# FFN-down of a decoder layer: one operand sum of a seven-product square made by a plain and an accumulating DMA into a ring, two operands in one subtraction, and 7, 7, 7, 5 such squares instead of 7, 7, 7, 4

## The chip, the core and the metric

The kernel runs on one NeuronCore of one Trainium2 chip. TensorE (PE) multiplies matrices, VectorE (DVE) and ScalarE (ACT) work elementwise, GpSimd (POOL) and SyncE (SP) issue transfers here, and 16 DMA engines move the bytes. The metric is device time of one launch in microseconds (us), lower is better. Matmuls accumulate in PSUM; everything else that is named below lies in SBUF.

## What is computed

One layer of a hybrid decoder for 256 tokens of width 2048, in float32: a mixer (multi-scale pooling beside RWKV-7), a squared-ReLU MLP of width 8192, a gate fed by a per-layer embedding, and a final norm. The change lies in the MLP's second product, and only there:

```python
h2 = rms_norm(x, mlp_norm[i])
x = x + jnp.square(jax.nn.relu(h2 @ w_ffn_up[i])) @ w_ffn_down[i]      # (256, 8192) @ (8192, 2048)

gate = jax.nn.sigmoid(rms_norm(x, ple_norm[i]) @ w_ple_gate[i])
x = x + gate * (p[i] @ w_ple_proj[i])
return rms_norm(x, final_norm)
```

## The kernel before, in words

**Two halves per operand.** Every float32 operand of a product is split into a rounded part and a rest (`split_sb`, L171; `halves_of`, L1233; `split_w`, L161): ACT copies it to the reduced matmul type, DVE subtracts that copy from the original. A product is then three matmuls (high by high, high by low, low by high), written by `prod` (L1225). All of them have a 128x128 stationary operand (activations) and a 128x512 moving operand (weights).

**Order of the work.** The FFN runs in two halves of 4096 hidden columns (`ffn_half`, L1302). Each half first makes eight activation tiles `y` (`gemm_wide`, L1098, lines L1112 and L1117), and then runs two sweeps (`down_sweep`, L1207), one for each 1024 output columns. A sweep visits 16 squares. A square is 256 rows of the weight by the 1024 columns of the sweep, seen as four 128x512 blocks w11, w12, w21, w22, against four 128x128 activation blocks a11, a21, a12, a22. The four sweeps are called d00, d01, d10, d11 here (half, then column pair).

**Plain and seven-product squares.** A plain square costs 8 products, 24 matmuls. A seven-product square (Winograd's form of Strassen's product, called a seven below) costs 7 products, 21 matmuls, but needs sums. The sums of activations, s1 to s4, are made once per half in `activation_sums` (L1191) and kept in the tiles `S`. The sums of weight blocks are made in each sweep: t1 = w12 - w11, t3 = w22 - w12, t2 = t3 + w11, t4 = w21 - t2, four DVE subtractions of 128x512 each (L1269 to L1272) into the tile `td`, and then split. The tuple `SEVEN` (L1188) names the seven odd squares that are done so in d00, d01 and d10; d11 has four of them, 1, 3, 7 and 11.

**Tiles and their buffers.** Weights come in by `load_raw` (L149) on the SP queue, two tiles `raw` of 512 KB per square, in six buffers (three of tag `raw`, three of `raw2`). The queue issues in order, so a load whose buffer isn't free holds those behind it. Split weights lie in three pairs of tiles `wh`, `wl`; a seven also uses one tile `wa` and two tiles of tag `graw`. In d11 four calls of `keep` (L1167, at the visits 5, 8, 11 and 14) load blocks of the next stage's gate weight, each through one of the same two `graw` tiles, and split them into tiles that are kept. Buffers of one tag are handed out in turn, in program order.

**Who sets the order.** In this part of the kernel the instructions are put in order by the compiler's list scheduler, by program order and by the `high_priority` sections; each engine then runs its list in order and waits at semaphores. POOL builds masks and moves tiles early in the program and does nothing in the FFN.

**After the last seven** of a sweep (L1284) DVE combines the banks of products 1, 5, 6, 7 into the residual `xr`, scaled by `s2`; in d11 half of the transposes of `xr` for the next stage follow there (`h3_part`).

Of the kernel before, what the change touches and what calls it, by code (L numbers as in the profile page):

```python
# [9 lines left out]
F32 = mybir.dt.float32  # L10
F32R = mybir.dt.float32r
# [29 lines left out]
def trunk(  # L41
# [1114 lines left out]
    def inv_ms():  # L1156
        ss2 = rms_stat(xr, "n2")
        nc.vector.tensor_scalar(s2, ss2, 1.0 / D, NORM_EPS, op0=ALU.mult, op1=ALU.add)
        nc.vector.reciprocal(s2, s2)

    h3_box = []

# [24 lines left out]

    SEVEN = (1, 3, 5, 7, 9, 11, 13)  # L1188
    s_slots = (0, 2, 5)

    def activation_sums(box, kp, r):  # L1191

        i = SEVEN.index(kp)
        if i % 2 == 0:
            st = a8(s_slots[i // 2], f"S{kp}", F32R) if i < 6 else fp.tile([128, 1024], F32R, tag="S", name=f"S{kp}")
# [6 lines left out]
        nc.vector.tensor_tensor(s3, a11, a21, op=ALU.subtract)  # L1202
        nc.vector.tensor_tensor(s2_, s1, a11, op=ALU.subtract)
        nc.vector.tensor_tensor(s4, a12, s2_, op=ALU.subtract)
        split_sb(st[:, 0:512], st[:, 512:1024], t_[:, 0:512])

    def down_sweep(hf, pair, ys, sboxes, hooks=(), between=None, seven=SEVEN):  # L1207

        nm = f"d{hf}{pair}"
        hooks = dict(hooks)  # L1210
# [12 lines left out]
        left = dict(todo)  # L1223

        def prod(n, a_, w_):  # L1225
            first, last = left[n] == todo[n], left[n] == 1
            left[n] -= 1
            (ah, al), (wh, wl) = a_, w_
            nc.tensor.matmul(banks[n], ah, wh, start=first, stop=False)  # L1229
            nc.tensor.matmul(banks[n], ah, wl, start=False, stop=False)  # L1230
            nc.tensor.matmul(banks[n], al, wh, start=False, stop=last)  # L1231

        def halves_of(src, name, own=False):  # L1233

            pool, kw = (fp, dict(bufs=2)) if own else (wp, {})
            wh = pool.tile([128, 1024], F32R, tag="graw" if own else "wh", name=f"wh_{name}", **kw)
            wl = pool.tile([128, 1024], F32R, tag="graw" if own else "wl", name=f"wl_{name}", **kw)
            with tc.high_priority(20000):
                for c in range(2):
                    nc.scalar.activation(wh[:, c * 512 : c * 512 + 512], src[:, c * 512 : c * 512 + 512], AF.Copy)  # L1240
                nc.vector.tensor_tensor(wl, src, wh.bitcast(F32), op=ALU.subtract)
# [6 lines left out]
        def add(tt, c, src):  # L1248
            nc.vector.scalar_tensor_tensor(xs(tt, c), src, s2[:, tt : tt + 1], xs(tt, c), op0=ALU.mult, op1=ALU.add)

        for q, kp in enumerate(((0, 2, 1, 4, 3, *range(5, 16)) if hf else (0, 2, 1, 4, 3, 6, 5, 8, 7, 10, 9, 12, 11, 14, 13, 15)) if pair else range(16)):
            if q in hooks:
                hooks[q]()
            y, j = ys[kp // 2], kp % 2 * 512
            a11, a21, a12, a22 = ((y[:, j + i * 128 : j + i * 128 + 128], y[:, 1024 + j + i * 128 : 1152 + j + i * 128]) for i in range(4))
            rx, ry = (load_raw(w_down[pair, hf * 32 + 2 * kp + i], 1024, f"{nm}_{kp}_{i}") for i in range(2))
            if kp in seven:
                i = SEVEN.index(kp)
                st = sboxes[kp][:, i % 2 * 1024 : i % 2 * 1024 + 1024]
                s1, s2_, s3, s4 = ((st[:, c * 128 : c * 128 + 128], st[:, 512 + c * 128 : 640 + c * 128]) for c in range(4))  # L1260
                t_ = a8(1, f"t{nm}_{kp}")
                t1, t3, t2, t4 = (t_[:, c * 512 : c * 512 + 512] for c in range(4))
                wa = fp.tile([128, 1024], F32R, tag="wa", name=f"wa{nm}_{kp}")
                w11 = wa[:, 0:512], wa[:, 512:1024]
                with tc.high_priority(20000):
                    split_sb(*w11, rx[:, 0:512])
                w21, w22 = halves_of(ry, f"{nm}_{kp}b")
                with tc.high_priority(20000):
                    nc.vector.tensor_tensor(t1, rx[:, 512:1024], rx[:, 0:512], op=ALU.subtract)  # L1269
                    nc.vector.tensor_tensor(t3, ry[:, 512:1024], rx[:, 512:1024], op=ALU.subtract)  # L1270
                    nc.vector.tensor_tensor(t2, t3, rx[:, 0:512], op=ALU.add)
                    nc.vector.tensor_tensor(t4, ry[:, 0:512], t2, op=ALU.subtract)  # L1272
                w1, w3 = halves_of(t_[:, 0:1024], f"{nm}_{kp}c")
                w2, w4 = halves_of(t_[:, 1024:2048], f"{nm}_{kp}d", True)
                for n, a_, w_ in (("1", a11, w11), ("2", a12, w21), ("3", s4, w22), ("5", s1, w1), ("7", s3, w3), ("6", s2_, w2), ("4", a22, w4)):
                    prod(n, a_, w_)
            else:
                w11, w12 = halves_of(rx, f"{nm}_{kp}a")
                for n, a_, w_ in (("2", a11, w11), ("4", a21, w11), ("3", a11, w12), ("x", a21, w12)):
                    prod(n, a_, w_)  # L1280
                w21, w22 = halves_of(ry, f"{nm}_{kp}b")
                for n, a_, w_ in (("2", a12, w21), ("4", a22, w21), ("3", a12, w22), ("x", a22, w22)):
                    prod(n, a_, w_)
            if kp == seven[-1]:  # L1284
                u = fp.tile([128, 512], F32, tag="r", bufs=2, name=f"u{nm}")
                with tc.high_priority(20000):
                    add(0, 0, b1)
                    nc.scalar.activation(u, b1, AF.Copy)
                    nc.vector.tensor_tensor(u, b6, u, op=ALU.add)
                    add(0, 1, b5)  # L1290
                    add(1, 1, b5)
                    add(0, 1, u)
                    nc.vector.tensor_tensor(u, b7, u, op=ALU.add)
                add(1, 0, u)
                add(1, 1, u)
                if between is not None:
                    between()
        for n, tt, c in (("2", 0, 0), ("4", 1, 0), ("3", 0, 1), ("x", 1, 1)):
            with tc.high_priority(30000):
                add(tt, c, banks[n])  # L1300

    def ffn_half(hf):  # L1302
# [26 lines left out]
        if hf == 0:  # L1329
            down_sweep(hf, 1, ys, sboxes)  # L1330
        else:
            down_sweep(hf, 1, ys, sboxes, {5: keep, 8: keep, 11: keep, 14: keep}, lambda: [h3_part("ple_norm", n) for n in range(2)], (1, 3, 7, 11))
# [9 lines left out]
    ph, pl = (fp.tile([128, 512], F32R, tag=nm, name=nm) for nm in ("ph", "pl"))  # L1342
    split_sb(ph, pl, praw[:, 0:512])
    pp = [a8(1 + tt, f"pp{tt}") for tt in range(2)]
    for n in range(4):
# [74 lines left out]
def _layout(i):  # L1420
# [13 lines left out]
    def ktiles(w):  # L1434
# [30 lines left out]
        "w_ffn_down": a["w_ffn_down"][0].reshape(64, 128, 2, 1024).transpose(2, 0, 1, 3),  # L1465
# [24 lines left out]
```

## Time and profile before

| what | value |
|---|---|
| runs of the kernel | 1180.1, 1182.39 and 1652.59 us, median 1182.39 |
| the execution that was profiled, its own time | 1180.25 us |
| its span from the first to the last instruction | 1178.2 us |
| DVE, ACT busy over the span | 873.3 us (74%), 709.3 us (60%) |
| sweeps d00 and d01, then d10 and d11, by TensorE's records | 557.9 to 722.5 us, 900.9 to 1069.6 us |
| sevens in the four sweeps | 7, 7, 7, 4 |

The profile is one execution. Its tables give busy time by engine, the span in 40 slices, the chain of work that ended last, groups of equal instructions, and waits with what ended them; a view by windows gives busy time of each engine in a stretch of the span, and a timeline lists the instructions of one engine with start, duration and, in brackets, the idle time ahead. A matmul of 128x512 is shown with 0.39 us, but matmuls are pipelined: what one costs in a full stream is the distance of two starts. Names with numbers left out stand for all tiles of that name (`raw_d` is every weight tile of FFN-down; `wl_d_6a` the low halves of the first weight tile of square 6).

### The profile page before, as it was taken

What the parts mean: (1) busy time and instruction counts of PE and PEld (TensorE: products, weight loads), DVE (VectorE), ACT (ScalarE), POOL (GpSimd) and SP (SyncE); (2) the same over time, 40 slices, a digit from 0 to 9 for tenths busy, and PEclk for the clock granted to TensorE, in tenths of its full rate; (3) what the DMA queues carried; (4) which work ended last, traced back from release to release, by engine and by line L of the source; (5) the groups of instructions that cost most, each with busy time, mean ns of one, the idle gap of its engine ahead of it and who ended that gap; (6) DMA issues with size and microseconds to landing.
All of it is one profiled execution on the core that took longest, in us unless ns stands there. A gap on an engine that the chain in (4) does not pass through costs nothing.

```text
span 1178.2 us, 17287 instructions
## 1 busy us (share of the span) xinstructions
PE 1162.5 (99%) x6419; PEld 973.4 (83%) x6419; DVE 873.3 (74%) x1188; ACT 709.3 (60%) x1309; POOL 13.7 (1%) x73
## 2 busy tenths in 40 slices
PE   8999999999999999999999999999999999999997
PEld 8787777788887888888888888888888888888886
DVE  7786996964656666767988987676668879788543
ACT  7776848676545565555665664555556655568543
POOL 2100000000000000000000000000000000000000
PEclk9999999999999999999999999999999999999999
DMA  7464343354465555555556556555555555767511
GB/s 290 154 202 146 135 140 119 119 179 157 160 203 178 177 182 196 184 192 200 187 204 212 198 202 209 186 191 191 185 195 190 202 205 195 290 233 249 197 56 72
DMA packets 60756, 216.81 MB, mean 184 GB/s; under 512 B 6784, under 2 KB 7552, under 8 KB 60288
## 3 DMA queue, kind: packets, MB, share of 16 engines
q1 hardware_dynamic: 60240, 214.99, 52.5%
q8 instruction: 50, 0.82, 0.3%
q10 hardware_dynamic: 432, 0.73, 0.2%
q14 instruction: 34, 0.28, 0.1%
HBM read 213.59 MB, written 2.10 MB: 183 GB/s over the span
## 4 chain that ended last, share of the span: by engine, by line
PE 96%; ACT 1%; DVE 1%; DMA 0%; issue 0%; SPq 0%; POOL 0%; DVEq 0%; POOLq 0%
PE u_w L1112 20%; PE u_w L1117 10%; PE d_b L1231 7%; PE d_b L1229 7%; PE d_b L1230 7%; PE d_w L1231 2%; PE d_w L1229 2%; PE d_w L1230 2%; PE gt_b L242 2%; PE gt_b L241 2%; PE gt_b L238 2%; PE zk_b L241 1%; PE zk_b L242 1%; PE o_b L241 1%; PE o_b L242 1%; PE zv_b L238 1%
## 5 line engine op out<-in xcount | busy, mean ns | idle before, releaser
L1112 PE MATMUL u_w<-h,wh_u 128*128 128x512 f32 x1024 | 321.9, 395 | 0.0
L167 ACT ACTIVATE wh_u<-raw_u 128x512 fp32r<-128x512 f32 x256 | 147.5, 623 | 160.9 <-issue 98.2
L168 DVE TENSOR_TENSOR wl_u<-raw_u,wh_u 128x1024 fp32r<-128x1024 f32 x128 | 156.6, 1224 | 105.2 <-ACT wh_u L167 103.5
L1117 PEld LDWEIGHTS u_w<-h,wl_u 128*128 128x128 f32 x1024 | 192.4, 188 | 45.4
L1117 PE MATMUL u_w<-h,wl_u 128*128 128x256 f32 x1024 | 201.4, 278 | 0.0
L1112 PEld LDWEIGHTS u_w<-h,wh_u 128*128 128x128 f32 x1024 | 156.0, 189 | 0.1
L168 DVE TENSOR_TENSOR wl_gt<-raw_gt,wh_gt 128x1024 fp32r<-128x1024 f32 x24 | 29.4, 1224 | 23.2 <-ACT wh_gt L167 23.2
L167 ACT ACTIVATE wh_gt<-raw_gt 128x512 fp32r<-128x512 f32 x48 | 28.0, 638 | 23.1 <-PE gt_b L242 14.4
L241 PE MATMUL gt_b<-wh_gt,h 128*128 128x512 f32 x96 | 37.3, 389 | 0.0
L242 PE MATMUL gt_b<-wh_gt,h 128*128 128x512 f32 x96 | 37.3, 389 | 0.0
L168 DVE TENSOR_TENSOR wl_o<-raw_o,wh_o 128x1024 fp32r<-128x1024 f32 x16 | 19.6, 1222 | 12.9 <-ACT wh_o L167 9.9
L167 ACT ACTIVATE wh_o<-raw_o 128x512 fp32r<-128x512 f32 x32 | 18.4, 623 | 16.3 <-issue 8.5
L167 ACT ACTIVATE wh_zp<-raw_zp 128x512 fp32r<-128x512 f32 x32 | 18.6, 623 | 15.7 <-PE zp_b L242 7.2
L168 DVE TENSOR_TENSOR wl_zk<-raw_zk,wh_zk 128x1024 fp32r<-128x1024 f32 x16 | 19.4, 1220 | 10.4 <-ACT wh_zk L167 10.4
L241 PE MATMUL zk_b<-wh_zk,hTh 128*128 128x512 f32 x64 | 25.2, 394 | 1.4 <-ACT wh_zk L167 1.4
L241 PE MATMUL zv_b<-wh_zv,hTh 128*128 128x512 f32 x64 | 26.0, 406 | 0.0
L167 ACT ACTIVATE wh_zk<-raw_zk 128x512 fp32r<-128x512 f32 x32 | 18.4, 622 | 12.4 <-PE zv_b L242 4.0
L241 PE MATMUL zp_b<-wh_zp,hTh 128*128 128x512 f32 x64 | 25.7, 401 | 0.0
L238 PE MATMUL gt_b<-wl_gt,h 128*128 128x512 f32 x96 | 25.7, 389 | 0.0
L168 DVE TENSOR_TENSOR wl_zv<-raw_zv,wh_zv 128x1024 fp32r<-128x1024 f32 x16 | 19.4, 1218 | 8.2 <-ACT wh_zv L167 7.4
L241 PE MATMUL zr_b<-wh_zr,hTh 128*128 128x512 f32 x64 | 25.4, 397 | 0.0
L242 PE MATMUL zp_b<-wh_zp,hTl 128*128 128x512 f32 x64 | 25.0, 391 | 0.0
(840 smaller groups left out, 2963.9 us busy)
## 6 DMA issues: line engine op xcount, KB each, us to landing
raw_u<-in_w_ffn_up_dram SPq DMA_DIRECT2D x128, 512.0 KB, 3.5
raw_d<-in_w_ffn_down_dram SPq DMA_DIRECT2D x128, 512.0 KB, 4.3
raw_gt<-in_w_ple_gate_dram SPq DMA_DIRECT2D x24, 512.0 KB, 3.5
raw_zk<-in_w_in_dram SPq DMA_DIRECT2D x16, 512.0 KB, 3.7
raw_zr<-in_w_in_dram SPq DMA_DIRECT2D x16, 512.0 KB, 3.3
raw_zv<-in_w_in_dram SPq DMA_DIRECT2D x16, 512.0 KB, 3.3
raw_zp<-in_w_in_dram SPq DMA_DIRECT2D x16, 512.0 KB, 3.2
raw_o<-in_w_out_dram SPq DMA_DIRECT2D x16, 512.0 KB, 4.2
```

Of the source, the lines that this page charges most:

```text
L167: nc.scalar.activation(wh[:, a * 512 : (a + 1) * 512], raw[:, a * 512 : (a + 1) * 512], AF.Copy)
L168: nc.vector.tensor_tensor(wl, raw, wh.bitcast(F32), op=ALU.subtract)
L238: nc.tensor.matmul(banks[tt], ah[:, ts_], halves[a][1], start=False, stop=last)
L241: nc.tensor.matmul(banks[tt], ah[:, ts_], halves[a][0], start=i + a == 0, stop=False)
L242: nc.tensor.matmul(banks[tt], al[:, ts_], halves[a][0], start=False, stop=False)
L1112: nc.tensor.matmul(bank[:, ct, :].rearrange("p (s t) -> p s t", s=2), wh[:, cs[ct]], hl, start=k == 0, stop=False, skip_group_check=True,)
L1117: nc.tensor.matmul(bank[:, ct, 0:T], wl[:, cs[ct]], hl[:, 0, :], start=False, stop=k == 15, skip_group_check=True)
L1229: nc.tensor.matmul(banks[n], ah, wh, start=first, stop=False)
L1230: nc.tensor.matmul(banks[n], ah, wl, start=False, stop=False)
L1231: nc.tensor.matmul(banks[n], al, wh, start=False, stop=last)
```

## The change

The output columns of index c = 1 are computed with the opposite sign inside a seven. Then the four weight operands are p1 = w11 + w12 (in place of t1), t2 = p1 - w22, and w21 - t2 and w11 - t2 (in place of t4 and t3). The last two are one subtraction over 1024 columns, with t2 broadcast, written in place over the weight tile `rx`, which now holds w21 and w11 side by side. The sign is put right when the banks are added to the residual (`ns2` = -`s2`, and s3 with its sign turned).

p1 isn't made by DVE. POOL issues two transfers of 256 KB into a slot of `ring` (four slots of 128x512): a plain one of w12, and one of w11 that adds to what is there. Both read the weight from HBM again. `begin_sum` issues them for the square that is four sevens ahead, at the end of each seven; the first four are issued ahead of the FFN. In turn the tile `ry` of a seven brings only w22 (256 KB).

The products of a seven go in the order 1, 2, 3, 5, 6, 4, 7 (before: 1, 2, 3, 5, 7, 6, 4). `wa` holds the split t2, the `graw` tiles the two results of the wide subtraction. d11 has five sevens, 1, 3, 5, 9 and 11, and visits the squares 0, 2, 1, 4, 3, 6, 5, 7, 8, and on to 15. The weight is laid out for these loads on the host. `S` for square 13 becomes a larger tile, in which `ph` and `pl` of the next stage lie too.

```diff
-    def down_sweep(hf, pair, ys, sboxes, hooks=(), between=None, seven=SEVEN):
+    ring = a8(1, "ring")
...
+            squares_of[hf, pair] = (1, 3, 5, 9, 11) if last else SEVEN
+            visits_of[hf, pair] = (0, 2, 1, 4, 3, 6, 5, 7, 8, *range(9, 16)) if last else (range(16), (0, 2, 1, 4, 3, 6, 5, 8, 7, 10, 9, 12, 11, 14, 13, 15))[pair]
+    in_line = [(*hp, kp) for hp, visits in visits_of.items() for kp in visits if kp in squares_of[hp]]
...
+    def slot(n):
+        return ring[:, n % 4 * 512 : n % 4 * 512 + 512]
+
+    def begin_sum():
+
+        n = len(begun)
+        if n < len(in_line):
+            hf, pair, kp = in_line[n]
+            nc.gpsimd.dma_start(slot(n), w_down[pair, hf * 16 + kp, 1, :, 1, :])
+            nc.gpsimd.dma_start(slot(n), w_down[pair, hf * 16 + kp, 0, :, 1, :], accum_op=ALU.add)
+            begun.append(n)
...
-            rx, ry = (load_raw(w_down[pair, hf * 32 + 2 * kp + i], 1024, f"{nm}_{kp}_{i}") for i in range(2))
+            rx, ry = (panel(kp, c, f"{nm}_{kp}_{c}", 1 if c and kp in seven else 2) for c in range(2))
             if kp in seven:
...
-                t_ = a8(1, f"t{nm}_{kp}")
-                t1, t3, t2, t4 = (t_[:, c * 512 : c * 512 + 512] for c in range(4))
+                p1 = summed(hf, pair, kp)
+                t2 = ry[:, 512:1024]
                 wa = fp.tile([128, 1024], F32R, tag="wa", name=f"wa{nm}_{kp}")
-                w11 = wa[:, 0:512], wa[:, 512:1024]
+                w2 = wa[:, 0:512], wa[:, 512:1024]
+                w21, w11 = halves_of(rx, f"{nm}_{kp}a")
+                wh, wl = (wp.tile([128, 1024], F32R, tag=hl, name=f"{hl}_{nm}_{kp}b") for hl in ("wh", "wl"))
+                w22, w1 = ((wh[:, c : c + 512], wl[:, c : c + 512]) for c in (0, 512))
                 with tc.high_priority(20000):
-                    split_sb(*w11, rx[:, 0:512])
-                w21, w22 = halves_of(ry, f"{nm}_{kp}b")
-                with tc.high_priority(20000):
-                    nc.vector.tensor_tensor(t1, rx[:, 512:1024], rx[:, 0:512], op=ALU.subtract)
-                    nc.vector.tensor_tensor(t3, ry[:, 512:1024], rx[:, 512:1024], op=ALU.subtract)
-                    nc.vector.tensor_tensor(t2, t3, rx[:, 0:512], op=ALU.add)
-                    nc.vector.tensor_tensor(t4, ry[:, 0:512], t2, op=ALU.subtract)
-                w1, w3 = halves_of(t_[:, 0:1024], f"{nm}_{kp}c")
-                w2, w4 = halves_of(t_[:, 1024:2048], f"{nm}_{kp}d", True)
-                for n, a_, w_ in (("1", a11, w11), ("2", a12, w21), ("3", s4, w22), ("5", s1, w1), ("7", s3, w3), ("6", s2_, w2), ("4", a22, w4)):
+                    split_sb(*w22, ry[:, 0:512])
+                    split_sb(*w1, p1)
+                    nc.vector.tensor_tensor(t2, p1, ry[:, 0:512], op=ALU.subtract)
+                    t43 = rx.rearrange("p (r n) -> p r n", r=2)
+                    nc.vector.tensor_tensor(t43, t43, t2.unsqueeze(1).to_broadcast([128, 2, 512]), op=ALU.subtract)
+                    split_sb(*w2, t2)
+                w4, w3 = halves_of(rx, f"{nm}_{kp}d", True)
+                for n, a_, w_ in (("1", a11, w11), ("2", a12, w21), ("3", s4, w22), ("5", s1, w1), ("6", s2_, w2), ("4", a22, w4), ("7", s3, w3)):
                     prod(n, a_, w_)
+                begin_sum()
...
+    for _ in range(4):
+        begin_sum()
     ffn_half(0)
     ffn_half(1)
```

More of the change, by code (lines that the diff above doesn't have):

```diff
@@ L1159, in inv_ms @@
         nc.vector.reciprocal(s2, s2)
+        nc.vector.tensor_scalar_mul(ns2, s2, -1.0)
     h3_box = []
@@ L1189, in trunk @@
     s_slots = (0, 2, 5)
+    ns2 = const.tile([128, 2], F32, name="ns2")
     def activation_sums(box, kp, r):
@@ L1205, in activation_sums, with summed, down_sweep @@
         split_sb(st[:, 0:512], st[:, 512:1024], t_[:, 0:512])
-    def down_sweep(hf, pair, ys, sboxes, hooks=(), between=None, seven=SEVEN):
+    ring = a8(1, "ring")
+    squares_of = {}
+    visits_of = {}
+    for hf in range(2):
+        for pair in range(2):
+            last = hf + pair == 2
+            squares_of[hf, pair] = (1, 3, 5, 9, 11) if last else SEVEN
+            visits_of[hf, pair] = (0, 2, 1, 4, 3, 6, 5, 7, 8, *range(9, 16)) if last else (range(16), (0, 2, 1, 4, 3, 6, 5, 8, 7, 10, 9, 12, 11, 14, 13, 15))[pair]
+    in_line = [(*hp, kp) for hp, visits in visits_of.items() for kp in visits if kp in squares_of[hp]]
+    begun = []
+    def slot(n):
[7 more added lines that the diff above has]
+            begun.append(n)
+    def summed(*square):
+        return slot(in_line.index(square))
+    def down_sweep(hf, pair, ys, sboxes, hooks=(), between=None):
         nm = f"d{hf}{pair}"
+        seven, visits = squares_of[hf, pair], visits_of[hf, pair]
         hooks = dict(hooks)
@@ L1246, in xs, with add, panel @@
             return xr[tt][:, o : o + 512]
-        def add(tt, c, src):
-            nc.vector.scalar_tensor_tensor(xs(tt, c), src, s2[:, tt : tt + 1], xs(tt, c), op0=ALU.mult, op1=ALU.add)
-        for q, kp in enumerate(((0, 2, 1, 4, 3, *range(5, 16)) if hf else (0, 2, 1, 4, 3, 6, 5, 8, 7, 10, 9, 12, 11, 14, 13, 15)) if pair else range(16)):
+        def add(tt, c, src, scale=s2):
+            nc.vector.scalar_tensor_tensor(xs(tt, c), src, scale[:, tt : tt + 1], xs(tt, c), op0=ALU.mult, op1=ALU.add)
+        def panel(kp, c, name, rows):
+            return load_raw(w_down[pair, hf * 16 + kp, c, :, 0:rows].rearrange("p r n -> p (r n)"), rows * 512, name)
+        for q, kp in enumerate(visits):
             if q in hooks:
@@ L1279, in down_sweep @@
-                for n, a_, w_ in (("2", a11, w11), ("4", a21, w11), ("3", a11, w12), ("x", a21, w12)):
+                w21, w11 = halves_of(rx, f"{nm}_{kp}a")
+                for n, a_, w_ in (("2", a12, w21), ("4", a22, w21), ("2", a11, w11), ("4", a21, w11)):
                     prod(n, a_, w_)
-                w21, w22 = halves_of(ry, f"{nm}_{kp}b")
-                for n, a_, w_ in (("2", a12, w21), ("4", a22, w21), ("3", a12, w22), ("x", a22, w22)):
+                w22, w12 = halves_of(ry, f"{nm}_{kp}b")
@@ L1283, in down_sweep @@
+                for n, a_, w_ in (("3", a12, w22), ("x", a22, w22), ("3", a11, w12), ("x", a21, w12)):
                     prod(n, a_, w_)
-            if kp == seven[-1]:
+            if kp == max(seven):
                 u = fp.tile([128, 512], F32, tag="r", bufs=2, name=f"u{nm}")
@@ L1291, in down_sweep @@
                     add(1, 1, b5)
-                    add(0, 1, u)
+                    add(0, 1, u, ns2)
                     nc.vector.tensor_tensor(u, b7, u, op=ALU.add)
                 add(1, 0, u)
-                add(1, 1, u)
+                add(1, 1, u, ns2)
                 if between is not None:
@@ L1341, in trunk @@
     praw = load_raw(pT.rearrange("p a t -> p (a t)"), 512, "pT")
-    ph, pl = (fp.tile([128, 512], F32R, tag=nm, name=nm) for nm in ("ph", "pl"))
+    phl = fp.tile([128, 2048], F32R, tag="S", name="phl")
+    ph, pl = phl[:, 0:512], phl[:, 512:1024]
     split_sb(ph, pl, praw[:, 0:512])
```

9 lines of the change are left out of this document (4 added, 5 removed).

## The prediction

> **What bounds the kernel now.** I read the page first, its busy shares and the chain, to see which engine sets the end; then TensorE's waits; then the windows of the four sweeps.
>
> ```profile
> PE 1162.5 (99%) x6419; PEld 973.4 (83%) x6419; DVE 873.3 (74%) x1188; ACT 709.3 (60%) x1309; POOL 13.7 (1%) x73
> ...
> PE   8999999999999999999999999999999999999997
> ...
> PE 96%; ACT 1%; DVE 1%; DMA 0%; issue 0%; SPq 0%; POOL 0%; DVEq 0%; POOLq 0%
> ```
>
> TensorE is busy in nearly every slice and is 96% of the chain. Busy time of pipelined matmuls can hide small gaps, so the waits and windows decide:
>
> ```profile
> PE zk_b L241 <- ACT wh_zk L167: 1.4, 1, 1.4
> ...
> PE um L854 <- ACT R L818: 0.4, 1, 0.4
> ...
> 557.90:640.20 82.30, 82.30 (x365) 68.18 (x364) 71.35 (x83) 49.66 (x86) 0.00 (x0) 1.00 0.58 202
> 640.20:722.50 82.30, 82.30 (x364) 68.12 (x363) 72.22 (x82) 49.12 (x85) 0.00 (x0) 1.00 0.57 199
> 900.90:983.20 82.30, 82.30 (x366) 68.14 (x365) 71.34 (x83) 49.64 (x86) 0.00 (x0) 1.00 0.55 197
> 983.20:1069.60 86.40, 86.40 (x389) 71.13 (x388) 73.19 (x83) 55.24 (x101) 0.00 (x0) 1.00 0.71 252
> ```
>
> TensorE has nine kinds of wait in the whole program, the first and the last are shown; none names `d_b` or `d_w`, the banks of FFN-down. In the windows (columns: length; busy of PE, weight loads, DVE, ACT, POOL; clock; DMA share; GB/s) TensorE is busy for all of each sweep at full clock, DVE for 72.22 of 82.30 us. So the sweeps last as long as their matmuls do. DVE relief is worth nothing by itself; only fewer matmuls are, as long as nothing new comes late.
>
> **The change, part by part.** The execution profiled took 1180.25 us; its span is 1178.2, and 2.05 lie around it. It is 2.1 under the median of the three runs shown (1182.39) and 0.15 over the lowest.
>
> *Matmuls: -0.69 us.* One square of d11 becomes a seven.
>
> ```profile
> 655.90 0.39 PE L1229 MATMUL d_b<-wh_d_4a,y 128*128 128x512 f32 x1
> ...
> 661.35 0.39 PE L1229 MATMUL d_w<-wad,y 128*128 128x512 f32 x1
> ...
> 666.11 0.39 PE L1229 MATMUL d_b<-wh_d_6a,y 128*128 128x512 f32 x1
> ...
> 671.54 0.39 PE L1229 MATMUL d_w<-wad,y 128*128 128x512 f32 x1
> ```
>
> The plain square 4 takes 661.35 - 655.90 = 5.45 us (24 matmuls, 0.227 each), the seven 3 takes 4.76 (21): 0.69 us less. It is on the path in full. All other squares keep their kind, and the order of products costs TensorE nothing.
>
> *DVE and ACT: 0, hidden under TensorE.* Steps of DVE in the stream:
>
> ```profile
> 663.27 1.22 DVE L1241 TENSOR_TENSOR wl_d_6a<-raw_d,wh_d_6a 128x1024 fp32r<-128x1024 f32 x1
> 664.40 0.68 DVE L173 TENSOR_TENSOR wad<-raw_d,wad 128x512 fp32r<-128x512 f32 x1
> 665.00 1.22 DVE L1241 TENSOR_TENSOR wl_d_6b<-raw_d,wh_d_6b 128x1024 fp32r<-128x1024 f32 x1
> 666.14 0.68 DVE L1272 TENSOR_TENSOR td<-raw_d,td 128x512 f32<-128x512 f32 x1
> ...
> L172 ACT ACTIVATE wad<-raw_d 128x512 fp32r<-128x512 f32 x25 | 15.4, 618 | 3.7 <-DMA raw_d<-in_w_ffn_down_dram 3.7
> ```
>
> A 512-wide step is 0.60 us, a 1024-wide one 1.14. A seven before: five narrow (four sums, one split) and three wide: 6.42. After: four narrow (t2, and the splits of w22, p1, t2) and three wide (w21 with w11, the double subtraction, its split): 5.82. That is -0.60 for 25 sevens, and +3.54 where a plain square (two wide, 2.28) becomes one: -11.5 us in all, off the path. The wide subtraction with a repeated operand isn't in the trace; I take 1.14 like other wide steps, between that and two narrow ones, 1.20, as a repeated operand brings no more elements. ACT keeps seven narrow copies per seven; the new seven adds three, 3 x 0.62 = 1.9 us, hidden: ACT is busy for 55.24 of 86.40 us in d11. `ns2` is one tiny step.
>
> The margin of DVE over TensorE is what hides this. `wl_d_6a` ends at 664.49 and is read by square 6's second matmul, 0.23 after 666.11: 1.85 us. A seven's first product now needs a wide split in place of a narrow one (+0.54), and its split w22 and p1 must follow the same buffer pair; TensorE stalls only where a chain is late by more than about 1.85.
>
> *More bytes: 0.* A seven loads 512 + 256 KB on SP and 2 x 256 KB on POOL in place of 1024 KB: +256 KB. A sweep of 16 squares goes from 16,384 to 18,176 KB, of which 7 x 256 = 1,792 KB accumulate. At the DMA share of d01 (0.57) that gives 0.63 if accumulating costs as much as copying. d11 already runs at 0.71 and 252 GB/s, and there TensorE has no gap either. So the added load is covered up to that point.
>
> No row shows an accumulating transfer or one issued by POOL. Below, its cost is 0 (hidden); no gain is possible, as the chain has no DMA in it. Above: the share without accumulating bytes stays 0.57, and these bytes add 0.57 x 1792/16384 = 0.062 for each multiple f of a copy's price; the engines are full at f = 6.9. I take hidden, as d11's row lies between.
>
> The Trainium skill (Collectives: The Full Stack, the part on the bandwidth ceiling) says that an adding transfer needs two source reads, so about twice the read traffic; by that f = 2, an estimate, the share is 0.69 and the sum stays as it is. No run here shows it yet.
>
> *Waits on POOL: 0.* The second transfer of a sum must wait until the first has landed, and the first until DVE and ACT have read the slot. POOL is at 0.00 in every sweep above and nothing else is queued there, so these waits hold only later sums. Who waits for them is ACT and DVE at p1, and behind it everything on these two engines. Sevens start 671.54 - 661.35 = 10.2 us apart, so four ahead is 41 us, less some 5 us of a seven's own time.
>
> ```profile
> raw_d<-in_w_ffn_down_dram SPq DMA_DIRECT2D x128, 512.0 KB, 4.3
> ...
> L158 SPq DMA_DIRECT2D raw_d<-in_w_ffn_down_dram x25: 327/328/328, 641.8 to 698.6; - x25
> ```
>
> Two transfers in a row at the price of twice the bytes, 4.3 us each, are 8.6: about 27 us to spare. The first four have the whole first half of the FFN.
>
> Against this the Trainium skill (SBUF — State Buffer, "Who interferes with whom") warns that transfers issued by GpSimd can starve while DVE holds the port they share, but by inference spares two-input subtractions like those here. If they were not spared, the writing of descriptors would have only DVE's idle 12% of d01: an issue of SP's 0.33 us would stretch to 2.7, two transfers to 14, still under 36. That is why the late sum below gets a small chance.
>
> *`rx` held longer: 0.* Before, `rx` was free after t2; now only after the split of w4 and w3, which product 4 needs.
>
> ```profile
> 664.51 0.33 SPq L158 DMA_DIRECT2D raw_d<-in_w_ffn_down_dram  x1
> ...
> 671.79 1.15 ACT L1240 ACTIVATE wh_d_8a<-raw_d 128x512 fp32r<-128x512 f32 x2 [1.56 <-issue]
> ```
>
> The load three squares on (square 8, behind seven 3) moves to at most 661.35 + 5 x 0.68 = 664.75; the next load behind it left at 664.51 anyway. Landing after 4.3, at 669.1, it is 2.7 us ahead of its split at 671.79.
>
> *`graw` and the kept gate weights: +1.75 us.* This is where I expect a new wait. In turn the two `graw` tiles go to seven 3, the first kept block, and the next seven. Before, that was square 7, two plain squares later; now it is square 5, one plain square later.
>
> ```profile
> 1008.84 0.39 PE L1231 MATMUL d_b<-wh_d_3d,y 128*128 128x512 f32 x1
> ...
> 1009.03 0.35 SPq L1170 DMA_DIRECT2D graw<-in_w_ple_gate_dram  x1
> ...
> 1016.20 1.15 ACT L1174 ACTIVATE gk<-graw 128x512 fp32r<-128x512 f32 x2 [0.29 <-DMA graw<-in_w_ple_gate_dram]
> ...
> 1018.64 1.23 DVE L1241 TENSOR_TENSOR wl_d_7d<-td,wh_d_7d 128x1024 fp32r<-128x1024 f32 x1
> ...
> DMA to landing us min/median/max: 4.0/5.1/7.1
> ```
>
> The kept load leaves as seven 3's last matmul ends (1009.03), lands 7.17 us later, and the low half of the next seven's pair, in the same tile, is ready at 1019.87, that is 3.67 after the landing. Counted from the end of seven 3: ready at 7.17 + 3.67 = 10.84. TensorE gets to that matmul after 5.45 for the plain square, five products of 0.68 and one matmul: 9.08. It waits 1.76 us. With the median landing of 5.1 the tile is ready at 8.77, and there is no wait. Bounds for one place: 0 (4.0 to 5.1) to 1.76 (7.1). It comes up twice, since seven 9, the third kept block and seven 11 stand alike. I take 1.75 for the first, whose load stood beside the 1 MB load of the final norm's weights and still will, and 0 for the other.
>
> Sum: 1180.25 - 0.69 + 1.75 = 1181.3 us.
>
> **The rivals.**
>
> *No stall at all.* If the scheduler hands `graw` over otherwise, or the first kept load lands in 5.1: 1180.25 - 0.69 = 1179.6. For it: TensorE had no wait in four sweeps. Against: the row at 1016.20.
>
> *The fifth square gives nothing and the chains get tight.* In place and behind p1, a seven's weights come later than the 1.85 us of margin allow, by some 0.2 us each: 26 x 0.2 = 5.2, on top of the forecast 1186.5. For it: two more dependent steps in a row, and ACT waiting in order. Against: DVE has 0.6 us more per seven.
>
> *Slower: accumulating transfers fill the DMA engines.* Place: the 16 engines in all sweeps; it decides from f = 6.9 on. At f = 10 a sweep of 82.3 us lacks (10 - 6.9) x 0.062 x 82.3 = 15.8 us, and with 26 sevens (3.7 sweeps' worth) 59 us: 1240. For it: no such row exists. Against: it needs seven times a copy's price.
>
> *Slower: sums late.* From about 36 us for one sum's two transfers on, each seven waits for the excess; at 40 us, 4 x 26 = 104 us: 1285. For it: POOL's path is untried here. Against: rows of 4.3 us.
>
> **How the numbers follow.** Forecast with a kept-block wait: 0.46. No stall: 0.26. Tight chains: 0.20. DMA engines full: 0.05. Sums late: 0.02. The remaining 0.01 is a scatter towards faster. About 2% (24 us) is what a measurement of this kernel can tell from no change. No case reaches 24 us less, since that would take a hundred matmuls: faster 0.01, same 0.92, slower 0.07. The predicted time is the forecast's, 1181.3. The range goes from the no-stall sum less the 2.3 us between the two close runs (1180.1, 1182.39), 1177.3, to the tight case plus as much, 1188.8; it holds 0.92 and its ends are the bounds of the unknown costs.
>
> **What the profile after would show.** Right: 369 matmuls of FFN-down in d11, distances of 0.227, PE waits of FFN-down of one or two entries on `wl_d_5d` or `wl_d_11d`, about 1.8 us; DVE near 68 of 82.3 us in d01; DMA share there 0.63 to 0.70; both transfers of a sum landed some 25 us before p1 is split. Wrong: waits of TensorE in d00, d01 or d10, a DMA share near 1, or ACT or DVE waiting for `ring`. A `graw` handed out in another order would take my 1.75 away.

## The result, and the profile after

The changed kernel takes 1199.83 us (median of four runs, 1196.25 to 1201.42) beside 1182.35 us for the kernel before on the same chip: a ratio of 1.015, 95% interval 1.0116 to 1.0184. It is slower by about 17 us, inside 2%, and outside the range that was forecast. One run of the kernel before (1652.59 us) and one of an experiment below (1442.19 us) were far slower than the rest, and no ratio uses them.

The profiled execution took 1198.61 us, span 1196.9. The busy shares and the first entries of the chain, as on the page of before:

```profile
PE 1168.4 (98%) x6416; PEld 972.9 (81%) x6416; DVE 859.4 (72%) x1169; ACT 707.0 (59%) x1312; POOL 51.2 (4%) x125
...
PE 17%; DVE 2%; DMA 1%; issue 1%; ACT 0%; DVEq 0%; SPq 0%; ACTq 0%
```

DVE is busy for 14 us less, ACT for 2 less, and POOL, which issues the sums, is busy for 4%. TensorE issues 3 matmuls fewer, yet is busy for 6 us more. And the chain, TensorE for 96% before, now runs over DVE and DMA as well and can be followed only for some 20% of the span. The waits of TensorE say where (us in total, times, longest):

```profile
PE d_b L1259 <- DVE wl_d_11d L1270: 2.6, 1, 2.6
PE d_b L1259 <- DVE wl_d_5b L173: 2.3, 2, 1.2
PE d_b L1259 <- DVE wl_d_11b L173: 2.3, 3, 1.0
PE d_b L1259 <- DVE wl_d_7b L173: 1.9, 1, 1.9
...
PE d_b L1259 <- DVE wl_d_3b L173: 1.4, 1, 1.4
...
PE d_w L1259 <- DVE wl_d_3b L173: 0.8, 1, 0.8
PE d_b L1259 <- DVE wl_d_5d L1270: 0.7, 1, 0.7
```

Where no bank of FFN-down stood before, eight kinds of entry stand now (the eighth, 0.3 on `wl_d_9b`, is left out). Most name `wl_..b` at L173: the low halves of w22 and p1. The windows of the four sweeps (columns as in the prediction):

```profile
557.67:644.50 86.83, 83.85 (x366) 67.67 (x364) 69.48 (x79) 49.01 (x87) 10.09 (x14) 1.00 0.70 215
644.50:730.10 85.60, 83.32 (x365) 67.86 (x364) 67.75 (x76) 48.64 (x86) 10.05 (x14) 1.00 0.70 220
908.40:994.56 86.16, 83.60 (x365) 67.76 (x364) 69.48 (x79) 49.04 (x87) 10.06 (x14) 1.00 0.69 217
994.56:1088.00 93.44, 88.59 (x391) 71.92 (x389) 73.68 (x84) 56.58 (x106) 1.43 (x2) 0.98 0.66 229
```

d00, d01 and d10 take 4.5, 3.3 and 3.9 us more than 82.3, and d11, up to the first matmul of the next stage, 93.4 where it took 86.9. That is 18.2 of the 18.7 us by which the span grew. TensorE isn't busy in all of these windows any more, and in d11 the clock is at 0.98.

The cause of the first three shows on DVE's timeline in d01 (start, length, and in brackets the idle time ahead with what ended it), in three stretches, with one row each of TensorE and SP:

```profile
676.29 0.69 DVE L1304 TENSOR_TENSOR raw_d<-ring,raw_d 128x512 f32<-128x512 f32 x1 [3.64 <-DMA raw_d<-in_w_ffn_down_dram]
676.90 1.22 DVE L1270 TENSOR_TENSOR wl_d_5d<-raw_d,wh_d_5d 128x1024 fp32r<-128x1024 f32 x1
678.03 0.68 DVE L173 TENSOR_TENSOR wl_d_5b<-raw_d,wh_d_5b 128x512 fp32r<-128x512 f32 x1
678.64 0.68 DVE L173 TENSOR_TENSOR wl_d_5b<-ring,wh_d_5b 128x512 fp32r<-128x512 f32 x1
...
678.77 0.50 PE L1259 MATMUL d_b<-wl_d_5b,S 128*128 128x512 f32 x1 [1.25 <-DVE wl_d_5b L173]
...
680.37 1.22 DVE L1270 TENSOR_TENSOR wl_d_8b<-raw_d,wh_d_8b 128x1024 fp32r<-128x1024 f32 x1
...
681.62 0.33 SPq L158 DMA_DIRECT2D raw_d<-in_w_ffn_down_dram  x1
...
686.59 0.69 DVE L1304 TENSOR_TENSOR raw_d<-ring,raw_d 128x512 f32<-128x512 f32 x1 [2.13 <-DMA raw_d<-in_w_ffn_down_dram]
687.20 1.22 DVE L1270 TENSOR_TENSOR wl_d_7d<-raw_d,wh_d_7d 128x1024 fp32r<-128x1024 f32 x1
```

L1304 is t2 = p1 - w22. The one at 676.29 belongs to seven 7, and behind it on DVE stand three splits of seven 5: the scheduler put the next seven's t2 ahead of them. t2 waits 3.64 us for its own load of w22; the splits behind it need nothing from that load, and TensorE waits 1.25 us for them. DVE runs its list in order: the Trainium skill (TensorE: Matmul & The Clock Gate, the part on the array's architecture) calls ACT's and DVE's queues strictly first in, first out, and these rows agree.

The stretch closes on itself. From t2 at 676.29 DVE works until the second tile of the plain square 8 is split, at 681.59. That split frees a buffer; SP issues the load of w22 for seven 9 into it at 681.62; it has landed when t2 of seven 9 starts, at 686.59. That is 5.30 of work and 4.97 of landing, 10.3 us in all, as long as TensorE needs for a pair of squares (10.2). There is no slack in the loop, so each late landing stays.

In the kernel before, the four sums stood behind all splits of the seven before them. DVE there, a view of the same kind:

```profile
670.27 1.23 DVE L1241 TENSOR_TENSOR wl_d_5c<-td,wh_d_5c 128x1024 fp32r<-128x1024 f32 x1 [1.18 <-ACT wh_d_5c L1240]
671.53 0.69 DVE L1269 TENSOR_TENSOR td<-raw_d 128x512 f32<-128x512 f32 x1
```

Those sums stood in a `high_priority` section as t2 does now, so the priority alone doesn't say why the scheduler moved t2 ahead; no run shows that.

Two more views of the changed kernel are needed later: transfers with their size and median landing, and groups of DVE and POOL (busy, mean ns of one, idle ahead).

```profile
raw_d<-in_w_ffn_down_dram SPq DMA_DIRECT2D x102, 512.0 KB, 4.4
ring<-in_w_ffn_down_dram POOLq DMA_DIRECT2D x52, 256.0 KB, 5.2
raw_d<-in_w_ffn_down_dram SPq DMA_DIRECT2D x26, 256.0 KB, 4.8
```

```profile
L1306 DVE TENSOR_TENSOR raw_d<-raw_d,raw_d 128x1024 f32<-128x1024 f32 x26 | 31.6, 1217 | 0.0
L1229 POOL DMA_DIRECT2D ring<-in_w_ffn_down_dram x26 | 22.6, 870 | 124.9 <-DMA ring<-in_w_ffn_down_dram 124.9
L1304 DVE TENSOR_TENSOR raw_d<-ring,raw_d 128x512 f32<-128x512 f32 x26 | 18.0, 691 | 44.3 <-DMA raw_d<-in_w_ffn_down_dram 44.1
L1228 POOL DMA_DIRECT2D ring<-in_w_ffn_down_dram x26 | 14.9, 575 | 597.6 <-DVE wl_d_1b L173 446.5 <-PE o3a_b L238 75.9 <-DVE wl_d_3b L173 19.5
```

t2 waited 44.1 us for its load over the program; the wide subtraction waits for nothing.

### The profile page after: what moved, and what is told of

Same layout as the page of the kernel before. It is cut to its first block, busy times and chain, and to the rows that moved or that the text cites. A ratio compares the mean times of both kernels' runs of the same rounds, so it can differ in the third digit from the quotient of the medians.

```text
span 1196.9 us, 17313 instructions
## 1 busy us (share of the span) xinstructions
PE 1168.4 (98%) x6416; PEld 972.9 (81%) x6416; DVE 859.4 (72%) x1169; ACT 707.0 (59%) x1312; POOL 51.2 (4%) x125
## 5 line engine op out<-in xcount | busy, mean ns | idle before, releaser
L1304 DVE TENSOR_TENSOR raw_d<-ring,raw_d 128x512 f32<-128x512 f32 x26 | 18.0, 691 | 44.3 <-DMA raw_d<-in_w_ffn_down_dram 44.1
L167 ACT ACTIVATE wh_gt<-raw_gt 128x512 fp32r<-128x512 f32 x48 | 27.8, 631 | 23.1 <-PE gt_b L242 14.4
L1228 POOL DMA_DIRECT2D ring<-in_w_ffn_down_dram x26 | 14.9, 575 | 597.6 <-DVE wl_d_1b L173 446.5
L1306 DVE TENSOR_TENSOR raw_d<-raw_d,raw_d 128x1024 f32<-128x1024 f32 x26 | 31.6, 1217 | 0.0
L1229 POOL DMA_DIRECT2D ring<-in_w_ffn_down_dram x26 | 22.6, 870 | 124.9 <-DMA ring<-in_w_ffn_down_dram 124.9
L168 DVE TENSOR_TENSOR wl_zk<-raw_zk,wh_zk 128x1024 fp32r<-128x1024 f32 x16 | 19.4, 1221 | 10.1 <-ACT wh_zk L167 10.1
```

Of the source, the lines that this page charges most:

```text
L167: nc.scalar.activation(wh[:, a * 512 : (a + 1) * 512], raw[:, a * 512 : (a + 1) * 512], AF.Copy)
L168: nc.vector.tensor_tensor(wl, raw, wh.bitcast(F32), op=ALU.subtract)
L1229: nc.gpsimd.dma_start(slot(n), w_down[pair, hf * 16 + kp, 0, :, 1, :], accum_op=ALU.add)
L1306: nc.vector.tensor_tensor(t43, t43, t2.unsqueeze(1).to_broadcast([128, 2, 512]), op=ALU.subtract)
```

## The experiments

They ran on three chips, each beside the kernel before, which took 1180.1 to 1180.4 us there; ratios are to it, with 95% intervals. Sweeps are lengths in us by TensorE's records, d11 up to the first matmul of the next stage.

| kernel | median us | ratio | d00 | d01 | d10 | d11 |
|---|---|---|---|---|---|---|
| before | 1180.25 | 1 | 82.3 | 82.3 | 82.3 | 86.9 |
| changed (with 1182.35 before) | 1199.83 | 1.015 (1.0116 to 1.0184) | 86.8 | 85.6 | 86.2 | 93.4 |
| t2 behind | 1184.76 | 1.0041 (1.0029 to 1.0054) | 82.3 | 82.3 | 82.3 | 90.7 |
| no sums | 1184.74 | 1.0040 (1.0025 to 1.0055) | 82.3 | 82.3 | 82.3 | 91.8 |
| traffic in before | 1182.82 | 1.0022 (1.0008 to 1.0036) | 82.9 | 83.0 | 82.3 | 93.2 |
| `rx` free | 1248.57 | 1.0576 (1.0560 to 1.0593) | 102.3 | 103.3 | 103.4 | 93.4 |
| t2 behind, kept moved | 1181.92 | 1.0011 (1.0002 to 1.0021) | 82.3 | 82.3 | 82.3 | 87.0 |
| t2 behind, four sevens | 1181.55 | 1.0007 (0.9998 to 1.0016) | 82.3 | 82.3 | 82.3 | 88.3 |
| kept moved alone | 1195.35 | 1.0120 (1.0105 to 1.0134) | 86.7 | 87.5 | 85.4 | 90.7 |
| t2 behind, six sevens | 1180.69 | 1.0000 (0.9992 to 1.0009) | 82.3 | 82.3 | 82.3 | 86.5 |
| six sevens, later transposes | 1181.04 | 1.0002 (0.9993 to 1.0011) | 82.3 | 82.3 | 82.3 | 87.1 |

### t2 behind the splits

t2 of a seven is placed on DVE behind the low half of p1 of the seven before. It moves by three places; nothing else on DVE, ACT or SP changes its place.

```diff
-                    split_sb(*w1, p1)
-                    nc.vector.tensor_tensor(t2, p1, ry[:, 0:512], op=ALU.subtract)
+                    w1_low = split_sb(*w1, p1)
+                    with tc.issue_after(w1_lows[-1].ins) if w1_lows else ExitStack():
+                        nc.vector.tensor_tensor(t2, p1, ry[:, 0:512], op=ALU.subtract)
+                    w1_lows.append(w1_low)
```

> The changed kernel, with t2 of a seven queued on DVE behind the last split (p1) of the seven before; nothing else moves on DVE, ACT or SP. Theory A (the scheduler placed t2 of the next seven ahead of three splits of the current one, and there DVE waits for the 256 KB load of w22 with the splits behind it): the 44.1 us of DVE waits at t2 fall under 10, TensorE's waits in d00, d01 and d10 go, each of these sweeps is within 1 us of 82.3, time 1180 to 1186. Theory B (the transfers on POOL slow the weight loads): waits stay, time 1194 or more. Theory C (rx held until w4 and w3 are split makes loads late): waits stay, time 1192 or more.

Measured: 1184.76 us, a ratio lower by 0.011 than the changed kernel's, 13 us. Three sweeps are back at 82.3. Of all the waits of TensorE on FFN-down one is left, in d11:

```profile
PE d_b L1260 <- DVE wl_d_11d L1271: 2.8, 1, 2.8
```

DVE no longer waits for any load of `raw_d`, and 256 KB on SP lands in 3.7 us where it took 4.8. So t2's place is a cause of the loss in the first three sweeps. `rx` is still held until w4 and w3 are split, and no wait follows from that.

### No sums

t2 stays ahead of the splits, but only the first four sums are transferred; the other 22 are left out, so their sevens work with old contents of the slots.

```diff
-                begin_sum()
```

> The changed kernel with only the first four sums transferred; all later sevens use one of these four, so the sums of the other 22 sevens are left out. The order on DVE, ACT and SP is that of the changed kernel. Theory B: the loads are quick again, time 1184 or less. Theory A: t2 still stands ahead of the splits and waits for w22; time 1192 to 1200, with TensorE's waits at the same places; a part of the waits may go if loads land somewhat sooner. Theory C: 1192 or more.

Measured: 1184.74 us, not the 1192 to 1200 of theory A, and the three sweeps are at 82.3 with t2 in the bad place. t2 still waits, but less, and TensorE doesn't:

```profile
DVE raw_d L1304 <- DMA raw_d<-in_w_ffn_down_dram: 13.7, 16, 1.8
```

Its transfers of 256 KB on SP land sooner:

```profile
raw_d<-in_w_ffn_down_dram SPq DMA_DIRECT2D x26, 256.0 KB, 3.6
```

t2 waits 13.7 us in place of 44.1, at most 1.8 at a time. With 3.6 of landing the loop above takes 5.3 + 3.6 = 8.9 us, under the 10.2 of a pair. So the place of t2 alone isn't enough: it takes the sums' traffic, which made this landing 4.8, too. That a wrong order alone makes the waits doesn't hold. Nor do the sums alone make the landing 4.8: with them and t2 behind it was 3.7.

d11 takes 91.8 here and keeps its wait, so that wait needs no sums:

```profile
PE d_b L1259 <- DVE wl_d_11d L1270: 2.7, 1, 2.7
```

### The traffic in the kernel before

The kernel before, with a plain and an accumulating transfer of 256 KB per seven into a spare tile that nobody reads, paced by a one-column copy on POOL.

```diff
+    def begin_sum(src, wa):
+
+        nc.gpsimd.tensor_copy(spare[:, 0:1], wa[:, 0:1].bitcast(F32))
+        nc.gpsimd.dma_start(spare, src[:, 512:1024])
+        nc.gpsimd.dma_start(spare, src[:, 0:512], accum_op=ALU.add)
...
+                begin_sum(w_down[pair, hf * 32 + 2 * kp], wa)
```

> The kernel before, with a plain and an accumulating 256 KB transfer added on POOL at each of its 25 sevens, into a tile that nothing reads (a one-column copy on POOL, of a tile that the seven has split, paces them). This is more traffic than in the changed kernel, since w12 and w22 are also loaded as before. Theory B: loads late, time 1192 or more. Theories A and C: hidden, 1180 to 1185.

Measured: 1182.82 us in the median, but spread from 1179.69 to 1187.94. The profiled execution was the slowest of them, with 93.2 us in d11; one wait stands out there, and the 512 KB loads land in 5.1 us (4.3 before):

```profile
PE d_b L1238 <- DVE wl_d_5a L1249: 2.8, 1, 2.8
```

```profile
raw_d<-in_w_ffn_down_dram SPq DMA_DIRECT2D x128, 512.0 KB, 5.1
```

Here each seven loads 1024 KB on SP and 512 on POOL, more than the changed kernel's 768 and 512. Traffic alone costs this kernel 0.2% in the median; it can't make the 1.5%. Single executions lose more, as the profiled one did, and no profile of a faster one exists.

### `rx` free after the subtraction

The wide subtraction writes into half of the ring in place of `rx`, so that the load behind can start earlier. The ring has two slots left, and sums are begun two sevens ahead.

```diff
-        return ring[:, n % 4 * 512 : n % 4 * 512 + 512]
+        return ring[:, n % 2 * 512 : n % 2 * 512 + 512]
...
+                    t43 = ring[:, 1024:2048].rearrange("p (r n) -> p r n", r=2)
+                    nc.vector.tensor_tensor(t43, rx.rearrange("p (r n) -> p r n", r=2), t2.unsqueeze(1).to_broadcast([128, 2, 512]), op=ALU.subtract)
...
-    for _ in range(4):
+    for _ in range(2):
```

> The changed kernel with the double subtraction written into half of the ring in place of over rx, so that rx comes free with t43; the ring keeps two slots, begun two sevens ahead. On DVE t2 still stands ahead of the splits of w22 and p1 of the current seven, and t43 has moved ahead of them too. Theory C: time 1186 or less. Theory A: t2 still waits with two splits behind it, time 1192 or more. Theory B: no change, or more, as sums are nearer to their use.

Measured: 1248.57 us. It tells nothing of `rx`, since the sums now come late:

```profile
DVE raw_d L1304 <- DMA ring<-in_w_ffn_down_dram: 79.1, 16, 6.5
...
POOL ring L1229 <- DMA ring<-in_w_ffn_down_dram: 128.3, 25, 6.5
```

From the first issue of a sum to its second landing the trace shows 10.7 us in the median (10.1 in the changed kernel). Two sevens ahead are 20 us, less the 10 by which t2 comes early: not enough. This is the late sum that the prediction had as a rival, at two slots; with four, DVE never waits for `ring`. Whether a sooner free `rx` helps with t2 in the early place stays open.

### The kept blocks, the number of sevens, and both

Four kernels, run together. The first holds t2 back and calls for the kept gate blocks at other visits of d11, so that none takes a `graw` tile between two close sevens:

```diff
-            down_sweep(hf, 1, ys, sboxes, {5: keep, 8: keep, 11: keep, 14: keep}, lambda: [h3_part("ple_norm", n) for n in range(2)])
+            down_sweep(hf, 1, ys, sboxes, {7: keep, 12: keep, 13: keep, 14: keep}, lambda: [h3_part("ple_norm", n) for n in range(2)])
```

> The changed kernel with t2 held behind the previous seven's p1 split (as in the run with t2 behind), and the four kept gate blocks of d11 moved from the visits 5, 8, 11, 14 to 7, 12, 13, 14, so that none takes a graw tile between two sevens that have only one plain square between them. Theory A (what is left in d11 of the run with t2 behind, 90.6 us against 86.9 before, is the hand-over of graw, first as a wait of 2.8 us on wl_d_11d, then as 3.4 us at half the clock): the wait goes, the clock stays, d11 takes about 86.2 us (86.9 less 0.69), total 1178.5 to 1180.5 beside 1180.1 for the kernel before. Rival B (the residue is the traffic of the sums, as in the run that put the traffic into the kernel before): a wait of 2 to 3 us on some weight tile of d11 stays, total 1182.5 to 1185. Rival C (the later kept blocks crowd the end of d11): a new wait on gk or the transposes behind d11, total 1182 to 1186.

The second holds t2 back and has d11's four sevens of the kernel before:

```diff
-            squares_of[hf, pair] = (1, 3, 5, 9, 11) if last else SEVEN
-            visits_of[hf, pair] = (0, 2, 1, 4, 3, 6, 5, 7, 8, *range(9, 16)) if last else (range(16), (0, 2, 1, 4, 3, 6, 5, 8, 7, 10, 9, 12, 11, 14, 13, 15))[pair]
+            squares_of[hf, pair] = (1, 3, 7, 11) if last else SEVEN
+            visits_of[hf, pair] = (0, 2, 1, 4, 3, *range(5, 16)) if last else (range(16), (0, 2, 1, 4, 3, 6, 5, 8, 7, 10, 9, 12, 11, 14, 13, 15))[pair]
```

> The changed kernel with t2 held behind the previous seven's p1 split, and d11 with the four sevens 1, 3, 7, 11 in the order of visits of the kernel before; everything else, the kept blocks too, as changed. Theory A (the fifth square costs what it does because it puts kept blocks between close sevens): no wait on a d tile, d11 about 86.9 us, total 1179.5 to 1181. Rival B (traffic of the sums makes the residue): a wait of 2 to 3 us on a weight tile of d11 with the halved clock behind it, total 1182.5 to 1185.

The third is the changed kernel with the kept blocks moved, and nothing else:

> The changed kernel with t2 where it was put (ahead of three splits of the seven before), only the kept blocks moved to the visits 7, 12, 13, 14. Theory A (two separate causes that add): d00, d01 and d10 stay at 86.8, 85.6 and 86.2 us, the wait on wl_d_11d goes and with it the halved clock, total 1193 to 1196 against 1199.8 for the changed kernel. Rival B (in d11 too the position of t2 is what counts): total stays within 1.5 us of 1199.8.

The fourth holds t2 back, has six sevens in d11 (1, 3, 5, 7, 9, 11) and the kept blocks at the visits 12 to 15:

> The changed kernel with t2 held behind the previous seven's p1 split, six sevens in d11 (1, 3, 5, 7, 9, 11, one plain square between each two), and the kept blocks behind all of them, at the visits 12 to 15. Theory A (nothing but graw and t2 holds TensorE): 0.69 us less than the run with five sevens and moved kept blocks, 1178 to 1180. Rival C (four kept blocks in four visits come late or their loads collide with the last weights): a wait on gk, h3t or a late weight of d11 of 2 us or more, total over 1182.

Measured: in the first, second and fourth no wait of TensorE on FFN-down is left and the clock is full. Windows of the first:

```profile
557.54:639.83 82.29, 82.29 (x365) 68.14 (x364) 70.74 (x79) 49.04 (x87) 10.09 (x14) 1.00 0.75 227
639.83:722.10 82.27, 82.27 (x364) 68.13 (x363) 68.86 (x76) 48.58 (x86) 10.04 (x14) 1.00 0.73 228
...
982.74:1069.80 87.06, 86.45 (x392) 71.11 (x390) 72.96 (x84) 56.13 (x104) 1.43 (x2) 1.00 0.70 232
```

With the DMA share of d01 at 0.73 TensorE is busy in all of it. Moving the kept blocks takes d11 from 90.7 to 87.0, and the time from 1184.76 to 1181.92. Alone (third kernel) it takes 0.3% off the changed kernel, 1195.35, within what was expected, but the intervals of the two overlap. In the profile d11 is 2.7 us shorter: the wait on `wl_d_11d` goes, those on `wl_..b` stay, and one of 2.3 us on `h` at the transposes comes in, with the clock halved behind it, which wasn't expected. Nor was a d01 of 87.5 in place of 85.6. So there are two causes, which nearly add.

The first kernel's median is over its expectation of 1178.5 to 1180.5, its profiled run (1179.62) within it; the second's is over by 0.5 us, with d11 at 88.3 where 86.9 was expected, 1.0 of it a wait for `h` at the transposes; the fourth's, 1180.69, is over its 1178 to 1180. Four, five or six sevens in d11 lie within 1.3 us of each other, where 1.4 us of matmuls lie between them. In the kernel with six, waits at the transposes behind the last seven take the place:

```profile
PE h3t L1134 <- DVE h L1141: 1.1, 1, 1.1
...
PE h3t L1134 <- DVE x L1279: 0.9, 1, 0.9
```

### Later transposes, and two more profiles

In the kernel with six sevens, the first half of the transposes is called for at the visit 14 in place of right behind the last seven.

```diff
-            down_sweep(hf, 1, ys, sboxes, {12: keep, 13: keep, 14: keep, 15: keep}, lambda: [h3_part("ple_norm", n) for n in range(2)])
+            down_sweep(hf, 1, ys, sboxes, {12: keep, 13: keep, 14: lambda: (keep(), [h3_part("ple_norm", n) for n in range(2)]), 15: keep})
```

> The kernel with six sevens in d11, with the first half of the transposes of xr called for at the visit 14 instead of right behind the last seven. In the run with six sevens the fifth and sixth square bring 1.4 us less matmul work, and the profile shows TensorE waiting 1.1 us for h and 0.9 us for the residual x at these transposes. Theory A (the gain of the squares is given back at the transposes): the first of these waits goes, the total is 0.7 to 1.2 us under the run with six sevens, 1179.5 to 1180, ratio to before 0.999. Rival B (the wait only moves to the transposes behind the sweep): the total stays within 0.5 us of 1180.7.

Measured: 1181.04 us, and a wait on `h` of 1.7 us in place of 1.1 and 0.9. The rival was right: the wait only moves. No version beats the kernel before; the best, six sevens with t2 behind, equals it (1.0000).

The kernel with t2 behind and the kept blocks moved was profiled twice more.

> A second profile of the kernel with t2 behind and the kept blocks moved; its twelve runs lay in two groups, 1179.6 to 1181.1 and 1182.7 to 1183.9 us, and the first profile was of the first. Theory A: if it falls into the second group, a wait of 2 to 3 us of TensorE on a weight tile of one sweep shows, as in the run that put the traffic of the sums into the kernel before. Rival B: no wait of TensorE in the sweeps in either group; the time lies elsewhere.

> A third profile of the same kernel, with the same expectations as the second: a TensorE wait on a weight tile in the sweeps if the time is over 1182.5 us (theory A), or none there (rival B).

They took 1181.44 and 1181.48 us; neither fell into the upper group. In both the first three sweeps take 82.3 and no weight tile is waited for; d11 takes 87.6 and 88.7, with waits for `h` of 0.7 and 1.2 us and, in the second, for `x` of 0.9. What the runs over 1182.7 us lose, no profile has shown: open.

## Why the prediction was wrong

TensorE waited in d00, d01 and d10, which the prediction had named as a sign that it is wrong. Term by term:

**Matmuls, -0.69: right.** From its first to its last matmul d11 took 86.24 us before and 85.93 with t2 behind and the kept blocks moved, in spite of 0.42 more at the transposes: 86.24 - 0.69 + 0.42 = 85.97.

**DVE and ACT, 0: the step that failed.** Its durations were right: the wide subtraction takes 1.217 us like other wide steps, and DVE is busy 14 us less (11.5 were worked out). What failed is that DVE's work was counted and its order wasn't asked for. The text had it that a seven's splits of w22 and p1 must follow the same buffer pair, and a margin of 1.85 us. It did not ask what the scheduler would put ahead of them. t2 went ahead of three splits that TensorE needs sooner, and it waits for a load, 44.1 us in all. Putting it back gains 13 us of the 17. The rival of tight chains named the right place, the weights of a seven, but another reason and 5.2 us.

**More bytes, 0: right about the engines, wrong about the landing.** The DMA share of d01 was forecast at 0.63 to 0.70 and is 0.73 at full speed of TensorE, so f = (0.73 - 0.57) / 0.062 = 2.6 (2.7 and 3.2 by d00 and d10, where the share is 0.75 and 0.74), far under 6.9. The 2 of the Trainium skill (Collectives: The Full Stack) is nearer than a copy's price. By the queues on the page of that run (t2 behind, kept blocks moved; packets, MB, share of the engines),

```profile
q1 hardware_dynamic: 60240, 208.17, 52.4%
q0 software_dynamic: 5824, 13.63, 5.5%
```

a MB of the sums' queue, half of it accumulating, costs 0.404 against 0.252, 1.6 times, which makes about 2.2 for accumulating if plain ones cost 1 (an estimate; that queue's packets are also smaller, 2.3 against 3.5 KB in the mean, and it doesn't tell the two apart). But the step asked only whether the engines fill. What counted was that a load of 256 KB took 4.8 us to land in place of 3.6 to 3.7, and that t2, at the head of DVE's list, handed that on to TensorE. The run without sums shows that without this traffic the order costs the first three sweeps nothing; the run with t2 behind shows that without the order this traffic costs the first three sweeps nothing.

**Waits on POOL, 0: right.** A sum takes 10.1 us in the median, 8.6 were worked out. Where it begins and is used in the same one of the first three sweeps, it has landed 29 to 32 us before its p1 is split (some 25 were forecast), and 19 to 22 before the early t2; four ahead is enough, and two, with t2 early, is not. An issue on POOL takes 0.575 and 0.870 us, not 2.7: what the Trainium skill (SBUF — State Buffer, "Who interferes with whom") warns of doesn't show beside these subtractions, which it spares by inference.

**`rx` held longer, 0: right with t2 behind**, where no load is late. In the changed kernel the split that frees `rx` stands behind t2 itself. In d00 and d01 SP's longest wait for it is 8.1 us there and 5.2 with t2 behind; after it the four loads of a pair leave within 3.5 us (678.14 to 681.62) in place of 4.6 (670.85 to 675.49). That this bunch makes the landing of 4.8 fits, but no run shows it alone.

**`graw` and the kept blocks, +1.75: right mechanism, wrong place and size.** The price was put on seven 5, with 0 for seven 11. In the changed kernel seven 5 waits 0.7 us and seven 11 2.6; with t2 behind it is less than 0.1 and 2.85. There the kept load landed 6.1 us after its issue, and the low half that TensorE needs came behind it on DVE (the same run, window of d11):

```profile
1043.76 1.23 DVE L1176 TENSOR_TENSOR gk<-graw,gk 128x1024 fp32r<-128x1024 f32 x1 [1.81 <-ACT gk L1175]
1044.91 1.22 DVE L1271 TENSOR_TENSOR wl_d_12a<-raw_d,wh_d_12a 128x1024 fp32r<-128x1024 f32 x1
1046.04 1.22 DVE L1271 TENSOR_TENSOR wl_d_11d<-raw_d,wh_d_11d 128x1024 fp32r<-128x1024 f32 x1
```

A split of the next square stands between them, 1.1 us that the step didn't count; and the wait halves the clock behind it (below). With t2 behind, moving the kept blocks gains 4.1 us from the first to the last matmul of d11 (90.06 to 85.93).

In sum, by one profile of each kernel: 14.4 us for t2's place (11.7 in three sweeps, 2.7 in d11), 4.1 for the kept blocks, less 0.7: 17.8 of 18.7, the rest at the transposes and behind.

## What to carry to other kernels

A busy share and a margin per step say nothing on an engine that runs its list in order: ask for each step that waits for a load what stands behind it. A loop of wait, split, free buffer, load and wait again has a period; add it up from the rows and compare it with that of the matmuls, with the landing that the new traffic will give. And where two tiles are shared by turns, count the plain work between two turns before squares are moved closer.

## What the hardware showed

A wait of TensorE can cost more than its length. Behind the wait in d11 the matmuls run at half speed for a while (the run with t2 behind; TensorE's timeline):

```profile
1044.08 0.39 PE L1259 MATMUL d_w<-wh_d_11d,S 128*128 128x512 f32 x1
1047.31 0.80 PE L1260 MATMUL d_b<-wl_d_11d,y 128*128 128x512 f32 x1 [2.85 <-DVE wl_d_11d L1271]
...
1048.33 0.63 PE L1260 MATMUL d_w<-wl_d_11d,S 128*128 128x512 f32 x1
1048.76 0.63 PE L1261 MATMUL d_w<-wh_d_11d,S 128*128 128x512 f32 x1
1049.19 0.63 PE L1259 MATMUL d_b<-wh_d_12a,y 128*128 128x512 f32 x1
...
1050.42 0.40 PE L1259 MATMUL d_b<-wh_d_12a,y 128*128 128x512 f32 x1
1050.66 0.39 PE L1260 MATMUL d_b<-wl_d_12a,y 128*128 128x512 f32 x1
```

```profile
1047.40:1050.40 3.00, 3.00 (x7) 2.39 (x8) 3.00 (x5) 0.60 (x1) 0.00 (x0) 0.51 0.87 277
```

Starts are 0.43 us apart in place of 0.227, and the granted clock is 0.51. Seven spacings take 3.11 us in place of 1.59, so the wait of 2.85 costs another 1.5. Over FFN-down and the transposes behind it in all 13 profiles, a distance of two starts up to 2.30 us was never followed by this, one of 2.91 or more always (14 of 14), and of three from 2.67 to 2.84 one was: 2.67, at the wait of 2.3 for `h` above. The Trainium skill (TensorE: Matmul & The Clock Gate, Part 1) states windows of about 3.4 us and warns of idle gaps above that; here somewhat shorter ones were enough, and the measurement decides.
